# New issue orders for all five engines, and one buffer for the residual's x and the attention output, in a hybrid attention layer

## The chip, the cores and the metric

The kernel runs on one core of a Trainium2 chip. The metric is the device time of one execution in microseconds (us), median of several runs.

## What is computed

One layer of a hybrid decoder for 256 tokens of 1024 channels, all float32. From the reference, cut to what matters here:

```python
h = _rmsnorm(x, norm1_g[i])
proj = h @ w_in[i]
(q_a, k_c, v_c, k_s, v_s, k_w, v_w, g_nsa,
 q_b, k_b, v_b, g_ma, g_mb) = jnp.split(proj, SPLIT_POINTS, axis=-1)
...
y_a = _nsa_mixer(q_a, k_c, v_c, k_s, v_s, k_w, v_w, g_nsa, ...)
y_b = _dilated_mixer(q_b, k_b, v_b)
mixed = jax.nn.sigmoid(g_ma) * (y_a @ w_o_a[i]) + jax.nn.sigmoid(g_mb) * (y_b @ w_o_b[i])
x = x + mixed @ w_out[i]
h2 = _rmsnorm(x, norm2_g[i])
x = x + jnp.square(jax.nn.relu(h2 @ w_up[i])) @ w_down[i]
```

## The kernel before

All products run on TensorE with a split into two parts: a value is a rounded high part plus a remainder, and a product is three matmuls, high by high, low by high and high by low. The activations' parts are hT0 and hT1 at the first norm. hT0 is x times the gain, made by ScalarE (L415), and hT1 is its remainder, made by VectorE (L416), both per 256 columns of the four x pieces xg0 to xg3, which each come by their own transfer; xg0 carries the gains too. The factor of the root mean square, rs, is applied later, to the products.

The weights come in pieces of 128 x 768 (384 KB; the four of kv_w are 128 x 840, and 420 KB). Each is transferred into a `raw` tile, on ScalarE's DMA queue for the first four (kv_c) and on SP's for all others (L315); ScalarE casts it to the high part wh (L345; the first one is cast by VectorE in two halves, L349), and VectorE subtracts for the low part wl (L350). A tile's number is written behind its name: wl_216 is the low part that belongs to raw_86 and wh_215. TensorE's products of the first projection chunks (accumulators acc_149, acc_150, then others) are at L468 and L479 to L481; those of the compression network (hacc) are at L613 and L615.

For rs, ScalarE squares the x pieces (sx, L426), GpSimd adds the squares (L428), TensorE sums over channels, VectorE writes ss (L435), and GpSimd raises it to the power -1/2 (L436). GpSimd also makes six rope tables from gr and rope (L444, L447). dg (L994) are diagonal matrices of rs. The first y tiles (L573) are products that ScalarE scales with rs. A key chunk goes through norm and rope on VectorE, which ends in vk (L524), and is transposed by TensorE in three matmuls (L552). y, 8 KB in each partition, also names the attention output, whose last part is read by ScalarE (L959) and VectorE (L960); x1 (L1101), another 8 KB, is x once more, for the residual after w_out (L1116).

What sets the order: the program is written in one order, and a table ORDER then gives for each of the five engines the sequence in which its instructions are issued, as numbers of the instructions as written ("0+4" is 0, 1, 2, 3); `issue_order` ties each to the one ahead of it, without a semaphore. Each engine runs its sequence strictly in order, so an instruction that waits holds all that stand behind it, and that holds for the transfers issued by SP too: at most eight transfers of the kernel are in flight, and a further one waits for the landing of one ahead. A tile from one of the pools `big`, `tok`, `att` and `ps` has a place of its own, whatever tag it is given, since the wrapper `Own` makes the tag unique:

```python
    def tile(self, shape, dt, name, **_):
        self.n += 1
        return self.pool.tile(shape, dt, name=name, tag=f"{name}{self.n}", bufs=1)
```

## Time and profile before

| | |
|---|---|
| three runs | 459.05, 459.05, 459.7 us, median 459.05 us |
| the profiled execution | 458.8 us, with a span of 457.0 us from its first to its last instruction |
| granted TensorE clock, mean | 0.993 |
| busy, of the span | TensorE 445.6 us, VectorE 358.0 us, ScalarE 284.2 us, GpSimd 83.7 us |
| read from memory | 75.28 MB |

Instructions of one engine are issued in order, and a row of the timeline shows when it began and for how long it was busy; consecutive ones overlap a little, so two of 0.96 us may take 1.8 us together. Matmuls are pipelined: of two that stand at 51.05 and 51.23 the pitch, 0.18 us, is the work, and 0.34 us is the time that one takes through the array. The time in brackets is how long the engine was idle ahead of the row, and on whom it waited. TensorE is the engine that sets the end, in the MLP alone for more than 200 us, which start with the products of L983 to L985.

### The profile page before, as it was taken

What the parts mean: (1) busy time and instruction counts of PE and PEld (TensorE: products, weight loads), DVE (VectorE), ACT (ScalarE), POOL (GpSimd) and SP (SyncE); (2) the same over time, 40 slices, a digit from 0 to 9 for tenths busy, and PEclk for the clock granted to TensorE, in tenths of its full rate; (3) what the DMA queues carried; (4) which work ended last, traced back from release to release, by engine and by line L of the source; (5) the groups of instructions that cost most, each with busy time, mean ns of one, the idle gap of its engine ahead of it and who ended that gap; (6) DMA issues with size and microseconds to landing.
All of it is one profiled execution on the core that took longest, in us unless ns stands there. A gap on an engine that the chain in (4) does not pass through costs nothing.

```text
span 457.0 us, 9071 instructions
## 1 busy us (share of the span) xinstructions
PE 445.6 (98%) x3413; PEld 431.1 (94%) x3413; DVE 358.0 (78%) x654; ACT 284.2 (62%) x622; POOL 83.7 (18%) x92
## 2 busy tenths in 40 slices
PE   4999999999999999999999999999999999999996
PEld 4999899899999999898999999999999999999996
DVE  3989999999999998899999886886856654555440
ACT  4855677678999778876775555665665634433330
POOL 2712121313041000200000001796322300000000
PEclk9799999999999999999999999999999999999999
DMA  8974586725535522541521647666666667677620
GB/s 304 367 244 146 154 287 181 236 89 167 157 105 141 171 70 71 175 140 68 162 82 42 199 128 231 201 193 186 205 184 195 183 187 210 185 216 199 179 78 13
DMA packets 29484, 76.92 MB, mean 168 GB/s; under 512 B 3664, under 2 KB 5120, under 8 KB 29312
## 3 DMA queue, kind: packets, MB, share of 16 engines
q1 hardware_dynamic: 28864, 74.77, 54.7%
q10 hardware_dynamic: 576, 1.57, 1.0%
q8 instruction: 27, 0.44, 0.4%
q14 instruction: 17, 0.14, 0.1%
HBM read 75.28 MB, written 1.05 MB: 167 GB/s over the span
## 4 chain that ended last, share of the span: by engine, by line
PE 93%; DVE 2%; ACT 2%; DMA 2%; issue 0%; ACTq 0%
PE acc L983 19%; PE acc L985 19%; PE acc L984 19%; PE acc L480 6%; PE acc L481 6%; PE acc L479 6%; PE tp L709 3%; PE acc L468 2%; DMA raw<-in_kv_c 2%; PE sp L754 1%; PE pvo L721 1%; ACT wh L345 1%; PE pvo L723 1%; PE tp L552 1%; PE dsp L920 1%; PE hacc L615 1%
## 5 line engine op out<-in xcount | busy, mean ns | idle before, releaser
L350 DVE TENSOR_TENSOR wl<-raw,wh 128x768 fp32r<-128x768 f32 (+2 forms) x183 | 177.6, 979 | 61.7 <-ACT wh L345 57.2
L345 ACT CAST wh<-raw 128x768 fp32r<-128x768 f32 (+1 forms) x182 | 149.6, 833 | 102.1 <-PE acc L984 74.5
L983 PE MATMUL acc<-u,wh 128*128 128x256 f32 x256 | 71.6, 280 | 0.0
L984 PE MATMUL acc<-u,wh 128*128 128x256 f32 x256 | 71.6, 280 | 0.0
L985 PE MATMUL acc<-u,wl 128*128 128x256 f32 x256 | 71.5, 279 | 0.0
L984 PE MATMUL acc<-h,wh 128*128 128x256 f32 x256 | 69.0, 280 | 0.0
L983 PE MATMUL acc<-h,wh 128*128 128x256 f32 x256 | 69.0, 279 | 0.0
L985 PE MATMUL acc<-h,wl 128*128 128x256 f32 x256 | 66.1, 279 | 0.0
L480 PE MATMUL acc<-wl,hT 128*128 128x384 f32 (+1 forms) x164 | 55.1, 350 | 0.3 <-DVE wl L350 0.3
L479 PE MATMUL acc<-wh,hT 128*128 128x384 f32 (+1 forms) x164 | 54.7, 348 | 0.0
L481 PE MATMUL acc<-wh,hT 128*128 128x384 f32 (+1 forms) x164 | 54.6, 347 | 0.0
L1159 POOL TENSOR_TENSOR r<-r 128x256 f32<-128x256 f32 x32 | 27.7, 866 | 128.7 <-ACT r L1158 127.5
L985 PEld LDWEIGHTS acc<-u,wl 128*128 128x128 f32 x256 | 48.2, 188 | 0.0
L983 PEld LDWEIGHTS acc<-u,wh 128*128 128x128 f32 x256 | 48.1, 188 | 0.0
L984 PEld LDWEIGHTS acc<-u,wh 128*128 128x128 f32 x256 | 48.1, 188 | 0.0
L983 PEld LDWEIGHTS acc<-h,wh 128*128 128x128 f32 x256 | 47.6, 188 | 0.0
L984 PEld LDWEIGHTS acc<-h,wh 128*128 128x128 f32 x256 | 47.4, 188 | 0.0
L985 PEld LDWEIGHTS acc<-h,wl 128*128 128x128 f32 x256 | 45.8, 188 | 0.0
L502 POOL TENSOR_TENSOR st<-st,nhalf 128x6 f32<-128x6 f32 (+1 forms) x16 | 21.6, 1348 | 92.8 <-DVE st L501 65.7
L984 PE MATMUL acc<-hT,wh 128*128 128x256 f32 x128 | 36.1, 293 | 0.0
L985 PE MATMUL acc<-hT,wl 128*128 128x256 f32 x128 | 35.9, 293 | 0.0
L983 PE MATMUL acc<-hT,wh 128*128 128x256 f32 x128 | 35.1, 290 | 0.0
(212 smaller groups left out, 986.9 us busy)
## 6 DMA issues: line engine op xcount, KB each, us to landing
raw<-in_cells SPq DMA_DIRECT2D x128, 384.0 KB, 3.4
raw<-in_cw SPq DMA_DIRECT2D x10, 384.0 KB, 3.2
raw<-in_q_a SPq DMA_DIRECT2D x8, 384.0 KB, 3.8
raw<-in_q_b SPq DMA_DIRECT2D x8, 384.0 KB, 3.4
raw<-in_k_b SPq DMA_DIRECT2D x8, 384.0 KB, 3.2
raw<-in_v_b SPq DMA_DIRECT2D x8, 384.0 KB, 3.1
raw<-in_kv_w SPq DMA_DIRECT2D x4, 420.0 KB, 6.7
raw<-in_kv_c ACTq DMA_DIRECT2D x4, 384.0 KB, 7.0
```

What stands on the lines that cost most here:

```text
L345: nc.scalar.copy(hi[:, :m], src)
L350: nc.vector.tensor_sub(lo[:, :m], src, f(hi[:, :m]))
L468: nc.tensor.matmul(acc[t][:, :n], hT[h][:, k, t * 128:(t + 1) * 128], w[:, kk * n:(kk + 1) * n], start=h == 0 and k == 0 and w is hi, stop ...
L479: nc.tensor.matmul(o, hT[0][:, k, ts], hi[:, c], start=k == 0, stop=False)
L480: nc.tensor.matmul(o, hT[0][:, k, ts], lo[:, c], start=False, stop=False)
L481: nc.tensor.matmul(o, hT[1][:, k, ts], hi[:, c], start=False, stop=k == 7)
L502: nc.gpsimd.tensor_tensor(st[:, 1, :h], st[:, 0, :h], nhalf[:, :h], op=OP.pow)
L709: nc.tensor.transpose(pt[0:rows, i * 128:(i + 1) * 128], s, ident)
L983: nc.tensor.matmul(o, hi, a[0][k], start=start, stop=False)
L984: nc.tensor.matmul(o, hi, a[1][k], start=False, stop=False)
L985: nc.tensor.matmul(o, lo, a[0][k], start=False, stop=stop)
L1159: mul = nc.gpsimd.tensor_mul(r, r, r)
```

## The change

Two things are changed. The tiles y and x1 now come from the pool directly, with the same tag and one buffer, so that they share a place; x1's transfer then has to wait for the last reader of y. And all five sequences of the table ORDER are replaced. The instructions themselves, their number as written included, are the same, except for that place. The core of the diff:

```diff
     "SP": """
-1 0 2 4 3 9+2 104 15 13 12 16 11 19 14 20 18 5 17 6 8 7 21+83 105+60 166 165 167+4 172 171 173+5 179 178
-180+4 185 184 186+4 191 190 192+5 198 197 199+2""",
+0+3 11 13 9 3 16 19 15 4 20 12 8 14 10 17 5 18 6+2 21+80 104 101+3 105+60 166 165 167+4 172 171 173+5 179
+178 180+4 185 184 186+4 191 190 192+5 198 197 199+2""",
     "ACT": """
-0+4 6 10 13 9 4+2 7+2 11 16 15 14 17 12 19+2 25+4 18 21 47 22 24 35 48 36 23 49 38 41 37 58 42 29+2 32+2 43
...
+0+4 5 4 9 8 7 10 6 15+2 11 13+2 25 19+2 12 26+2 17 28 23 18 24 21 54 29 22 35 32+2 36 30 47 38 58 31 50 48+2
...
     "DVE": """
-3 2 4+2 12 0+2 6+2 13+2 16 22 18 15 19 23 8+3 24+2 17 11 77 79 20 58 21 36 59 37 60 64+2 62 66 39 61 47 63
...
-    st_["y"] = once([128, 8, S], F32, "y")
+    st_["y"] = big.pool.tile([128, 8, S], F32, name="y", tag="y", bufs=1)
...
-    x1 = big.tile([128, 8, S], F32, name="x1", tag="y", bufs=1)
+    x1 = big.pool.tile([128, 8, S], F32, name="x1", tag="y", bufs=1)
     nc.sync.dma_start(x1.rearrange("p k s -> p (k s)"), A["xg"][:, 16:])
```

Twelve lines fewer stand in the table after, so a line of the program after is the line before less 12.

**The start, on ScalarE and VectorE.** ScalarE, behind the four transfers of kv_c that it issues, before:

```order
L345 CAST wh_160<-raw_83 128x768
L426 ACTIVATE sx1_181<-xg1_77 128x512
L345 CAST wh_215<-raw_86 128x768
L426 ACTIVATE sx0_180<-xg0_76 128x512
L415 ACTIVATE hT0_137<-xg0_76 128x256 x2
L415 ACTIVATE hT0_137<-xg1_77,xg0_76 128x256 x2
L426 ACTIVATE sx2_182<-xg2_78 128x512
L415 ACTIVATE hT0_137<-xg2_78,xg0_76 128x256 x2
```

After:

```order
L403 ACTIVATE hT0_137<-xg0_76 128x256 x2
L414 ACTIVATE sx0_180<-xg0_76 128x512
L403 ACTIVATE hT0_137<-xg1_77,xg0_76 128x256 x2
L414 ACTIVATE sx1_181<-xg1_77 128x512
L333 CAST wh_160<-raw_83 128x768
L403 ACTIVATE hT0_137<-xg2_78,xg0_76 128x256 x2
L414 ACTIVATE sx2_182<-xg2_78 128x512
L333 CAST wh_215<-raw_86 128x768
```

VectorE at its start, before:

```order
L349 CAST wh_155<-raw_80 128x384 x2
L350 TENSOR_TENSOR wl_156<-raw_80,wh_155 128x768
L350 TENSOR_TENSOR wl_161<-raw_83,wh_160 128x768
L350 TENSOR_TENSOR wl_216<-raw_86,wh_215 128x768
L416 SCALAR_TENSOR_TENSOR hT1_138<-xg0_76,hT0_137 128x256 x2
L416 SCALAR_TENSOR_TENSOR hT1_138<-xg1_77,xg0_76,hT0_137 128x256 x2
L350 TENSOR_TENSOR wl_220<-raw_89,wh_219 128x768
```

After:

```order
L404 SCALAR_TENSOR_TENSOR hT1_138<-xg0_76,hT0_137 128x256 x2
L337 CAST wh_155<-raw_80 128x384 x2
L338 TENSOR_TENSOR wl_156<-raw_80,wh_155 128x768
L404 SCALAR_TENSOR_TENSOR hT1_138<-xg1_77,xg0_76,hT0_137 128x256 x2
L338 TENSOR_TENSOR wl_161<-raw_83,wh_160 128x768
L404 SCALAR_TENSOR_TENSOR hT1_138<-xg2_78,xg0_76,hT0_137 128x256 x2
L338 TENSOR_TENSOR wl_216<-raw_86,wh_215 128x768
```

On ScalarE the scalings (hT0) of xg0 and xg1 moved ahead of the casts and the squares; on VectorE the remainders (hT1) of xg0 moved to the head, those of xg1 ahead of wl_161 and wl_216, and those of xg2 ahead of wl_216 and wl_220.

**The transfers that SP issues first.** Before:

```order
L314 DMA xg1_77<-in_xg 128x512
L314 DMA xg0_76<-in_xg 128x528
L314 DMA xg2_78<-in_xg 128x512
L315 DMA raw_92<-in_kv_s 128x768
L314 DMA xg3_79<-in_xg 128x512
L315 DMA raw_102<-in_kv_w 128x840
L381 DMA gr_104<-in_gr 128x768
L1101 DMA x1_3396<-in_xg 128x2048
L393 DMA cw2_114<-in_cw2 128x256
```

After:

```order
L302 DMA xg0_76<-in_xg 128x528
L302 DMA xg1_77<-in_xg 128x512
L302 DMA xg2_78<-in_xg 128x512
L372 DMA rope_106<-in_rope 128x256
L377 DMA rowm_110<-in_rowm 128x1
L303 DMA raw_102<-in_kv_w 128x840
L302 DMA xg3_79<-in_xg 128x512
L303 DMA raw_116<-in_kv_w 128x840
```

x1 (1024 KB) stood eighth; it now stands behind 101 others, three places ahead of where it is written, with weight pieces before and behind it. gr, which all rope tables need, went from seventh to sixteenth, and xg0 from second to first.

**The transposes of the key tile vk_439, on TensorE, and the end of vk_439 on VectorE.** hT0_137 is x's high part, blk1_375 the input of the compression network, tp_614 the transposed tile. TensorE before:

```order
L480 MATMUL acc_578<-wl_413,hT0_137 128x384
L481 MATMUL acc_578<-wh_412,hT1_138 128x384
L479 MATMUL acc_578<-wh_482,hT0_137 128x384
L480 MATMUL acc_579<-wl_519,hT0_137 128x384
L552 MATMUL tp_614<-ident_100,vk_439 128x128 x3
L480 MATMUL acc_578<-wl_483,hT0_137 128x384
L552 MATMUL tp_722<-ident_100,vk_571 128x128 x3
```

After:

```order
L467 MATMUL acc_763<-wh_826,hT0_137 128x384
L601 MATMUL hacc_811<-wh_816,blk1_375 96x256
L603 MATMUL hacc_811<-wl_817,blk1_375 48x256
L467 MATMUL acc_764<-wh_685,hT0_137 128x384
L601 MATMUL hacc_811<-wh_816,blk1_375 96x256
L603 MATMUL hacc_811<-wl_817,blk1_375 48x256
L540 MATMUL tp_614<-ident_100,vk_439 128x128 x3
L601 MATMUL hacc_811<-wh_816,blk1_375 96x256
```

VectorE before:

```order
L350 TENSOR_TENSOR wl_501<-raw_394,wh_500 128x768
L350 TENSOR_TENSOR wl_519<-raw_416,wh_518 128x768
L524 TENSOR_TENSOR vk_439<-t1_434,st_430 128x384
L524 TENSOR_TENSOR vk_571<-t1_566,st_562 128x384
L350 TENSOR_TENSOR wl_581<-raw_418,wh_580 128x768
```

After:

```order
L621 TENSOR_TENSOR z0_780<-tp_777,z1_781 128x96
L499 TENSOR_TENSOR t1_734<-t1_734,t2_735 128x384
L338 TENSOR_TENSOR wl_817<-raw_677,wh_816 128x768
L623 SCALAR_TENSOR_TENSOR z1_781<-z1_781,z0_780 128x96
L512 TENSOR_TENSOR vk_439<-t1_434,st_430 128x384
L338 TENSOR_TENSOR wl_827<-raw_689,wh_826 128x768
```

Before, tp_614 is the 231st of TensorE's matmuls in the trace (a transpose is one, the ten at the start are counted) and vk_439 the 78th step of VectorE; after, the 319th and the 96th. The matmuls and steps between moved ahead of them.

## Rows read from the trace of the kernel before

**Rows 1.** The page, part 1: busy us (share of the span) xinstructions.

```profile
PE 445.6 (98%) x3413; PEld 431.1 (94%) x3413; DVE 358.0 (78%) x654; ACT 284.2 (62%) x622; POOL 83.7 (18%) x92
```

**Rows 2.** The chain of waits from 0 to 13 us: start us, us, what.

```profile
1.65 7.63 DMA raw<-in_kv_c
...
9.30 0.83 ACT wh L345
10.13 0.53 ACT sx L426
10.66 0.41 ACT hT L415
```

**Rows 3.** The timeline from 4.5 to 12 us: start, us, instruction [idle before <-releaser].

```profile
5.01 0.63 DVE L349 CAST wh<-raw 128x384 fp32r<-128x384 f32 x2 [5.01 <-DMA raw<-in_kv_c]
...
6.98 0.19 POOL L440 COPY g<-xg 128x8 f32<-128x8 f32 x1 [4.58 <-DMA xg<-in_xg]
...
7.52 0.83 ACT L345 CAST wh<-raw 128x768 fp32r<-128x768 f32 x1 [3.39 <-DMA raw<-in_kv_c]
...
11.12 1.33 PE L468 MATMUL acc<-wh,hT 128*128 128x384 f32 x3 [4.09 <-ACT hT L415]
```

**Rows 4.** DMA issues up to 1.15 us: KB each, median us to landing.

```profile
xg<-in_xg SPq DMA_DIRECT2D x1, 256.0 KB, 4.1
```

**Rows 5.** Stretches, all engines: us, busy (instructions) of each engine, granted clock, DMA.

```profile
11.10:17.10 6.00, 5.98 (x18) 5.64 (x19) 6.00 (x8) 6.00 (x12) 4.10 (x3) 0.50 1.04 389
17.10:24.00 6.90, 6.90 (x44) 6.81 (x43) 6.87 (x10) 3.58 (x5) 5.63 (x7) 1.00 0.98 345
```

**Rows 6.** Stretches, VectorE alone: us, busy (instructions), granted clock, DMA.

```profile
5.00:11.10 6.10, 3.48 (x6) 0.93 1.02 394
11.10:52.70 41.60, 40.01 (x76) 0.93 0.68 224
52.70:140.00 87.30, 84.90 (x181) 1.00 0.60 181
```

**Rows 7.** The timeline of TensorE, 49 to 53 us.

```profile
49.66 0.28 PE L613 MATMUL hacc<-wh,blk 128*96 128x256 f32 x1
49.78 0.28 PE L615 MATMUL hacc<-wl,blk 128*48 128x256 f32 x1
...
51.05 0.34 PE L481 MATMUL acc<-wh,hT 128*128 128x384 f32 x1
51.23 0.34 PE L479 MATMUL acc<-wh,hT 128*128 128x384 f32 x1
51.87 0.44 PE L480 MATMUL acc<-wl,hT 128*128 128x384 f32 x1 [0.30 <-DVE wl L350]
52.42 0.52 PE L552 MATMUL tp<-ident,vk 128*128 128x128 f32 x3
```

**Rows 8.** The timeline of VectorE before those transposes.

```profile
49.99 1.81 DVE L350 TENSOR_TENSOR wl<-raw,wh 128x768 fp32r<-128x768 f32 x2
51.73 1.01 DVE L524 TENSOR_TENSOR vk<-t,st 128x384 f32<-128x384 f32 x2
```

**Rows 9.** The timeline of GpSimd, five of the rope tables.

```profile
18.44 5.24 POOL L444 TENSOR_TENSOR ropeg<-rope,gr 128x256 f32<-128x256 f32 x5 [1.26 <-DMA rope<-in_rope]
```

**Rows 10.** The timeline of VectorE beside GpSimd's sums and tables.

```profile
15.95 2.99 DVE L350 TENSOR_TENSOR wl<-raw,wh 128x768 fp32r<-128x768 f32 x2
18.86 2.73 DVE L416 SCALAR_TENSOR_TENSOR hT<-xg,xg,hT 128x256 fp32r<-128x256 f32 x3
21.52 1.57 DVE L350 TENSOR_TENSOR wl<-raw,wh 128x840 fp32r<-128x840 f32 x1
...
23.70 3.10 DVE L350 TENSOR_TENSOR wl<-raw,wh 128x840 fp32r<-128x840 f32 x3
```

**Rows 11.** The timeline: VectorE's last read of y; ScalarE's cast behind x1's place.

```profile
244.93 0.43 DVE L960 SCALAR_TENSOR_TENSOR yb<-y,yb 128x256 fp32r<-128x256 f32 x1 [0.48 <-ACT yb L959]
...
253.96 0.84 ACT L345 CAST wh<-raw 128x768 fp32r<-128x768 f32 x1
```

More of the change, by code (lines that the diff above doesn't have):

```diff
@@ L120 @@
     "SP": """
-1 0 2 4 3 9+2 104 15 13 12 16 11 19 14 20 18 5 17 6 8 7 21+83 105+60 166 165 167+4 172 171 173+5 179 178
-180+4 185 184 186+4 191 190 192+5 198 197 199+2""",
+0+3 11 13 9 3 16 19 15 4 20 12 8 14 10 17 5 18 6+2 21+80 104 101+3 105+60 166 165 167+4 172 171 173+5 179
+178 180+4 185 184 186+4 191 190 192+5 198 197 199+2""",
     "ACT": """
[15 rows of a table removed]
-474 473 475+3 479 478 481 480 482 484 483 485+3 489 488 491 490 492 494 493 495+3 499 498 501 500 502+38""",
-    "DVE": """
[20 rows of a table removed]
-635+2 634 637+4 643 641 644 642 645+4 650+2 649 652+2""",
-    "PE": """
[60 rows of a table removed]
-2575+17 2597 2592+3 2598 2595 2599+20 2620 2619 2621+767""",
[15 rows of a table added]
+495+3 499 498 501 500 502+38""",
+    "DVE": """
[20 rows of a table added]
+650+2 649 652+2""",
+    "PE": """
[48 rows of a table added]
+1870+2 1893+3 1899+4 1872 1896 1903+4 1873+2 1897+2 1907+1481""",
     "POOL": """
-28 25 2 15 14 0+2 7 3+3 11+2 10 9 8 6 13 18 17 16 19+3 23+2 22 26+2 34+2 38 37 40 29 39 30 33 31 36 32 42 41
-45+5 44 50+5 56 55 57+4 62 61 63+11 43 74+14""",
+15 14 28 25 1 0 2 7 3+3 13 12 11 6 9 8 10 18+2 16+2 20+2 23 22 24 26+2 34+2 38 29 39 30 37 40 33 36 31+2
+41+11 53 52 54+34""",
 }
```

175 rows, old and new, of the table ORDER are left out of this document.

## The prediction

> **What bounds the kernel now.** I read the page's busy times first, then the chain of waits over the start, then the timeline there, then stretches of busy time, then the places further on where TensorE waits. TensorE is busy for 445.6 us of the 457.0 us span [rows 1]; so 11.4 us of the span are not TensorE work, and no change of order alone can win more. The profiled execution took 458.8 us, that is 1.8 us outside the span and 0.25 us under the median of the three runs (459.05). I make the sum on 458.8 and carry the difference to the median.
>
> Most of the 11.4 us is the start. The chain from the first issue to the first real matmul is a weight transfer (kv_c) to 9.28, then ScalarE's cast of it, then a square of x, then the first hT0 scaling, and then the matmul [rows 2]: ScalarE's queue holds hT0 of xg0, which is all that the first matmul lacks, behind two casts and two squares. The timeline shows that none of this is needed: xg0 had landed by 6.98 (GpSimd's small copy starts then), VectorE had cast the first weight piece at 5.01, ScalarE sat idle for 3.39 us until a weight at 7.52, and TensorE idled 4.09 us until 11.12 [rows 3]. A second loss follows: after this idle time the granted clock was 0.50 (1.2 GHz) from 11.10 to 17.10, so TensorE started 18 matmuls in 6.00 us, against 44 in 6.90 us at 1.00 (2.4 GHz) [rows 5]. At full rate 18 matmuls of 0.18 us (one starts at 51.05, the next at 51.23 [rows 7]) are 3.2 us, so 2.8 us went there, and TensorE stands as if it had started at 13.9 with the full clock.
>
> The other bound is VectorE, which makes the low half (wl) of every weight and hT1. It did only 3.48 us of work in six instructions before 11.1, and then 40.01 us in 41.60 [rows 6]: from the start to 52 us it is nearly always busy, and TensorE runs on what it hands over. The place that shows it is 51.87, where TensorE waits for a wl, and 52.42, the transposes of vk [rows 7], which VectorE finished only just before (two wl from 49.99, two vk from 51.73 [rows 8]). Past it VectorE is idle 2.4 us of 87.3 [rows 6], so it is close but no longer last.
>
> **The change, part by part.** *ScalarE's and VectorE's start.* hT0 and hT1 of xg0 now stand first on both engines, and xg0 is the first transfer on SP. The first transfer there took 4.1 us from its issue at 0.73 [rows 4], so xg0 lands at about 4.8; at worst at 6.98 as before [rows 3]. From 4.8, ScalarE's two hT0 (0.41 each by the chain [rows 2]) end at 5.7; VectorE's two hT1 (0.91 each, three took 2.73 [rows 10]) run to 7.3, its two half casts (0.63 [rows 3]) to 7.9. The first half cast is there at 7.6, so the first real matmul moves from 11.12 to about 7.6. The matmuls that follow use hT1 and wl in the order in which VectorE now makes them: wl of the first piece (0.87) to 8.8, hT1 of xg1 to 10.6, one wl, hT1 of xg2 to 13.2, three wl, the first hT1 of xg3 at 16.9. The product with that last one has 8.0 us of TensorE work ahead of it in the new order (matmuls counted in the order, 0.18 us each), so TensorE then stands as if started at 8.9 instead of 13.9: 5.0 us better. The low clock does not add to it: even if another 18 matmuls took 6.0 us [rows 5], the same count gives 10.8 at most, which the next step exceeds.
>
> *What VectorE lets through.* It is last further on, so its own lead counts. By 11.1 it will have done two hT1, the two half casts, one wl, two more hT1 and half a wl: 1.8 + 0.6 + 0.9 + 1.8 + 0.5, about 5.6 us, against 3.48 [rows 6]: 2.1 us ahead. It gives some back: its dg (from rs) now stand ahead of two wl, and ScalarE's first y likewise waits for rs ahead of a cast. rs needs GpSimd's pow after ss, which VectorE writes at about 22, so the two engines stand for about 2.0 us there; before, VectorE lost about 1.6 us in all between 11.1 and 52.7 (41.60 - 40.01 [rows 6]), which now falls away in part. I take 0.3 to 0.5 us as the net price, 0.4; if rs came in time it would be nothing. The lead is then 1.7 to 1.8 us.
>
> *The tight place.* The transposes of vk_439 (52.42 [rows 7]) go back on TensorE past 44 matmuls of 384 columns at 0.18 us (51.05 to 51.23 [rows 7]) and 39 of 256 columns at 0.12 us (49.66 to 49.78 [rows 7]): 7.7 + 4.7 = 12.4 us of work that no longer waits for them. On VectorE vk_439 goes back past nine wl and nine smaller steps. Two wl take 1.74 us from start to start (49.99 to 51.73 [rows 8]), so nine are 7.8; the nine are up to 0.50 each (two vk took 1.01 [rows 8]), with three short ones, 3.3 us in all. 12.4 - 11.1 = 1.3 us more room. Other products there (wl for the compression matmuls, the next transposes) have, by the same count, nearly the same room, so no more than this comes. Lead and room, 1.8 + 1.3, make 3.1 us, less than the 5.0 that the start gives: **-3.1 us** to the region about 50 us.
>
> *From 100 to 140.* There the new order puts projections closer behind their wl than the old one: counted the same way, the smallest room of VectorE against TensorE is 1.3 us less than before. Before, TensorE was some 2 us behind what VectorE allowed there (VectorE's idle time is 2.4 us [rows 6]); with 3.1 us gained, 1.8 of them VectorE's own, about 0.5 us falls back: **+0.5**, between 0 and 1.5. From 140 to 250 the small rearrangements of transposes and attention steps move instructions by a few places; TensorE had short waits there in both directions, and I take 0, within 1.5 either way. The MLP is in written order in both and its part is equal.
>
> *x1 in y's buffer.* The 1 MB transfer leaves the start, where it stood eighth on SP; at 389 GB/s [rows 5] it had delayed all behind it by 2.7 us, which brings the kv_w weights forward. It now waits for y's last reader, VectorE's yb at 244.93 + 0.43 [rows 11], and holds the cell weights queued behind it on SP. Issued at about 242.6 with the gain, it takes some 2.7 us, and the 384 KB behind it 1.1 us more: 246.4, some 247 with the issue. ScalarE casts that piece at 253.96 [rows 11], about 251 with the gain. Four us of cover: **0**. If the cover were gone, each us late would cost one.
>
> *Rest.* GpSimd's tables and sums beside VectorE's wl. Before, a table took 1.05 us (5.24 for five [rows 9]); beside them one wl of 840 columns took 1.57 us against 1.03 alone (3.10 for three), and a pair beside a sum took 2.99 where 1.9 was due [rows 10]: 0.5 and 1.1 us lost. In the new order three or four wl stand beside tables, at 0.5 us each, so 1.5 to 2.0 against 1.6: 0, within 1.
>
> The sum is -3.1 + 0.5 = -2.6 us: 456.2 on the profiled execution, **456.4 us** on the median.
>
> **The rivals.** *A: the start's gain is kept whole.* If VectorE's wl pass 52 us with no new waits and the 0.3 us waits of [rows 7] simply vanish, TensorE runs 4.5 to 5.0 us ahead: 454.2. For it: the new order is spread so that VectorE has wl for other products between. Against it: VectorE's 40.01 of 41.60 busy [rows 6], which leaves no reserve to win more than its own lead. *B: VectorE blocked by GpSimd.* If a wl is held for a whole table (1.05 us) instead of half, three of them lose 3.2 instead of 1.6 us, and the gain shrinks to about 1.0: 458.0. Against it: 0.5 us for the row of 1.57 [rows 10]; for it the pair of 2.99. The Trainium skill, page "SBUF — State Buffer", section "Who interferes with whom", says just this: a VectorE instruction with two SBUF inputs contends with a GpSimd instruction that reads SBUF, and the later one is fully blocked; by that rule the time would be B's, and the trace agrees only for part of the cases. *C: xg0 lands no earlier.* Moved to the head of SP it may still share the 16 engines with the four kv_c weights; landing at 6.98 it takes 2.1 us from VectorE's lead, which leaves 3.1 - 2.1 + 0.5: 458.5. Against it: the 4.1 us of the first transfer [rows 4]. *D, slower: rs comes late.* gr, which the tables need, is sixteenth on SP instead of seventh. Some 5.5 MB are queued up to it, at 389 GB/s 14.1 us, so it lands at about 18, and three tables (0.7 + 2 x 1.05) and the pow end before 22, when ss comes anyway. ScalarE's y and VectorE's dg wait on rs with all casts and wl behind them. Each us that rs is past 23.5 then costs one us of lead; with 3.1 us gained it turns to slower past about 26.5, that is, if gr landed after about 23. At rs 28 the time would be 460.5. Against it: the rates of 389 and 345 GB/s [rows 5], which would have to fall by a third.
>
> **How the numbers follow.** The forecast, -1.5 to -4 us, has 0.57; A 0.16; B and C 0.08 each; D 0.11. Less than 0.2%, 0.9 us, cannot be told from no change here. Half of B and C lies within it. So faster is 0.57 + 0.16 + 0.06, some 0.78, same 0.11, slower 0.11. The range goes from A's better end, 453.9, to C with its own uncertainty, 458.9, and leaves out D and the far end of A.
>
> **What would show it.** The first real matmul at about 7.6; VectorE's hT1 from about 5.4 and 5 to 6 us of work before 11.1; xg0 landed by 5; TensorE at vk_439's transposes about 3 us earlier for the same work; rs at about 23; x1 issued at about 242 and the cast behind it without idle time. I am wrong if TensorE waits longer than 1 us anywhere past 60 us, if rs is later than 26, or if VectorE's wl beside tables take 2 us.

## The result, and the profile after

The changed kernel takes 463.03 us (median of four runs, 462.92 to 463.3) against 459.05 us before (458.94 to 459.7): 1.0085 times as long, with an interval of 1.0067 to 1.0102. It is slower by 4.0 us, where 456.4 was predicted. Its profiled execution took 462.92 us; the view of the cores gives its span and granted clock, which is higher than before (0.993):

```profile
core 0: 461.1 us, clock 0.999
```

The beginning went as meant. The timeline from 4 to 14 us (start, us, instruction, in brackets the idle time ahead and its releaser) answers to [rows 3]:

```profile
5.22 0.91 ACT L403 ACTIVATE hT<-xg 128x256 fp32r<-128x256 f32 x2 [0.93 <-DMA xg<-in_xg]
...
5.77 0.89 DVE L404 SCALAR_TENSOR_TENSOR hT<-xg,hT 128x256 fp32r<-128x256 f32 x2 [5.77 <-ACT hT L403]
...
6.57 0.62 DVE L337 CAST wh<-raw 128x384 fp32r<-128x384 f32 x2
...
7.07 1.65 PE L456 MATMUL acc<-wh,hT 128*128 128x384 f32 x8 [0.58 <-DVE wh L337]
```

xg0 had landed by 5.22, VectorE began with hT1 at 5.77, and the first real matmul stands at 7.07 instead of 11.12. In the stretches of [rows 5] (us, busy time and instructions of TensorE, its weight loads, VectorE, ScalarE and GpSimd, granted clock, DMA share, GB/s) the half clock is gone:

```profile
11.10:17.10 6.00, 5.41 (x29) 4.48 (x28) 6.00 (x7) 4.69 (x8) 2.46 (x2) 1.00 1.05 386
17.10:24.00 6.90, 6.90 (x41) 6.81 (x42) 6.23 (x8) 1.64 (x3) 3.16 (x5) 1.00 0.92 320
```

In those of VectorE alone, which answer to [rows 6], it had done 5.30 us of work by 11.1 instead of 3.48:

```profile
5.00:11.10 6.10, 5.30 (x9) 1.00 1.04 404
11.10:52.70 41.60, 39.63 (x70) 1.00 0.70 232
```

So the gain was made and then lost. To see where, I take TensorE's **lateness**: the start of a matmul in the trace, less the work of all real matmuls that stand ahead of it in that kernel's order, each at its usual pitch at full clock. An engine that never waits keeps its lateness; each wait, each slow stretch adds to it. Since the two orders differ, "at 50 us" means after 50 us of work, and no particular matmul.

| us of TensorE work done | lateness before | after | difference |
|---|---|---|---|
| 0 | 11.12 | 7.07 | -4.1 |
| 20 | 14.11 | 9.60 | -4.5 |
| 30 | 14.19 | 11.21 | -3.0 |
| 50 | 15.59 | 13.33 | -2.3 |
| 100 | 16.19 | 14.57 | -1.6 |
| 140 | 16.80 | 17.21 | +0.4 |
| 250 | 23.19 | 24.08 | +0.9 |
| 300 | 23.66 | 24.92 | +1.3 |
| 420 | 24.73 | 29.05 | +4.3 |

The usual pitch of a shape is not one number, and the rows are good to about half a us: with the median pitch of each shape over both traces the differences are -4.5 at 20, -3.3 at 30, -2.3 at 50, -1.5 at 100, +1.2 at 140 and +0.6 at 250.

Three losses stand in it: 2.2 us from 20 to 50, 3.2 us from 50 to 250 (most of it from 100 to 140), 3.4 us from 250 to the end. A matmul at the same place in both programs says much the same without the table: the 1821st, in the residual's projection, began at 269.10 before and at 269.61 after, and the last one, in the down projection, at 452.86 and 457.00.

**The first loss** shows on VectorE, in two places. The first is beside GpSimd's tables. GpSimd's timeline after, with rs between two groups of tables:

```profile
17.99 0.59 POOL L435 TENSOR_TENSOR ropeg<-ropec,gr 48x128 f32<-48x128 f32 x1 [1.36 <-DMA gr<-in_gr]
18.54 1.44 POOL L432 TENSOR_TENSOR ropeg<-rope,gr 128x256 f32<-128x256 f32 x2
22.83 0.72 POOL L424 TENSOR_TENSOR rs<-ss,nhalf 128x2 f32<-128x2 f32 x1 [2.85 <-DVE ss L423]
23.51 2.14 POOL L432 TENSOR_TENSOR ropeg<-rope,gr 128x256 f32<-128x256 f32 x3
```

VectorE's timeline at the same time:

```profile
17.23 5.45 DVE L338 TENSOR_TENSOR wl<-raw,wh 128x840 fp32r<-128x840 f32 x4
...
23.59 1.46 DVE L982 TENSOR_SCALAR dg<-ident,rs 128x128 f32<-128x128 f32 x2 [0.63 <-POOL rs L424]
24.96 1.50 DVE L338 TENSOR_TENSOR wl<-raw,wh 128x768 fp32r<-128x768 f32 x1
```

Four wl took 5.45 us, two dg 1.46 and one wl 1.50. The view of the tile wl gives the four one by one (ns, shortest/median/longest):

```profile
L338 DVE TENSOR_TENSOR wl<-raw,wh x4: 947/1020/2694, 17.2 to 21.7; 128x840 fp32r<-128x840 f32 x3, 128x768 fp32r<-128x768 f32 x1
```

Three took 0.95 to 1.02 us, as a wl does with GpSimd idle, and one, which began at 18.17, took 2.69: GpSimd made three tables in a row from 17.99 to 19.97, and the wl did some 0.9 us of work behind them. The kernel before pays the same way, in other instructions. Three hT1 beside its tables (view of the tile hT):

```profile
L416 DVE SCALAR_TENSOR_TENSOR hT<-xg,xg,hT x3: 953/959/972, 18.9 to 20.6; 128x256 fp32r<-128x256 f32 x3
```

Two hT1 with GpSimd idle, at the start of the kernel after:

```profile
L404 DVE SCALAR_TENSOR_TENSOR hT<-xg,hT x2: 482/484/485, 5.8 to 6.2; 128x256 fp32r<-128x256 f32 x2
```

Added up from 5 to 28 us, what VectorE's instructions take beyond the time of their kind with GpSimd idle is 5.7 us before (3.1 beside sums, 2.6 beside tables) and 6.4 after (3.2 and 3.2). So this costs a lot in both kernels, and the new order added 0.7 us to it.

The second place stands in VectorE's timeline at 47.67, an idle time of 1.12 us:

```profile
47.67 0.96 DVE L338 TENSOR_TENSOR wl<-raw,wh 128x768 fp32r<-128x768 f32 x1 [1.12 <-ACT wh L333]
```

The chain of waits (start, us, what) says why:

```profile
41.24 0.96 DVE wl L338
42.25 4.45 DMA raw<-in_cw
46.81 0.84 ACT wh L333
```

ScalarE could not cast before a weight of the compression network, issued at 42.25, had landed at 46.7; and the chain puts ahead of that issue a wl of VectorE itself, which ended at 42.20. So it is a loop from VectorE over the transfer and ScalarE back to VectorE. In VectorE's own lateness (its time less its own work) the lead over the kernel before was about 3.4 us at 12 us of work, 2.0 at 20, 1.9 at 35 and 0.9 at 40.

**The second loss** has no large wait. The view of waits lists only one past 50 us, of 0.4 us, and it is in TensorE's timeline (384 columns have a pitch of 0.18 us here, so the second row is 0.56 us late):

```profile
124.63 0.34 PE L469 MATMUL acc<-wh,hT 128*128 128x384 f32 x1
125.36 0.51 PE L709 MATMUL pvo<-phi,vSW 128*128 128x512 f32 x1 [0.39 <-ACT P L769]
```

From 94 to 142 us of the trace the matmuls that start over 0.1 us late sum to some 2.6 us after and 0.7 us before; with the smaller ones the difference is 2.7 to 3.2 us, by the pitch that is taken as usual. TensorE is idle for only 0.56 us of it (not at all before), so how much is waiting and how much TensorE's own change from one shape to the next is not told apart here.

**The third loss** is in the MLP, where nothing waits at all. Both kernels have 120 us of TensorE work in 120 us, at a granted clock of 1.00, but not the same number of matmuls. The row of this stretch before (each count holds two that were already running at 320.00):

```profile
320.00:440.00 120.00, 120.00 (x1028) 120.00 (x1027) 69.61 (x90) 58.15 (x92) 13.89 (x18) 1.00 0.67 191
```

And after:

```profile
320.00:440.00 120.00, 120.00 (x1002) 120.00 (x1002) 67.33 (x87) 56.30 (x90) 14.20 (x17) 1.00 0.69 193
```

The pitch of equal matmuls, fp32r and 256 columns wide, is 117.06 ns in the mean before (mostly 116.67) and 120.0 ns after. A pitch is a mean here: at 120.0 every start is 120 ns behind the one ahead, at 116.67 they lie 113 to 120 ns apart. In the kernel after it changes at one place, the two float32 matmuls of the second norm (L1155; L1167 before). TensorE's timeline after, around it:

```profile
311.16 0.28 PE L973 MATMUL acc<-h,wl 128*128 128x256 f32 x1
...
312.45 0.28 PE L972 MATMUL acc<-h,wh 128*128 128x256 f32 x1
...
312.69 0.59 PE L1155 MATMUL tp<-sqs,ones 128*128 128x256 f32 x2
...
313.24 0.28 PE L972 MATMUL acc<-h,wh 128*128 128x256 f32 x1
...
314.56 0.28 PE L971 MATMUL acc<-h,wh 128*128 128x256 f32 x1
```

Eleven pitches take 1.29 us ahead of it (311.16 to 312.45), which is 117 ns each, and 1.32 us behind it (313.24 to 314.56), 120 ns each, and so it stays for 1198 matmuls: 1198 x (120.0 - 117.06) ns = 3.5 us.

**x1** did not wait for y. The rows of its line:

```profile
L1089 SPq DMA_DIRECT2D x<-in_xg x1: 328/328/328, 233.7 to 233.7; - x1
...
DMA to landing us min/median/max: 4.7/4.7/4.7
```

And VectorE's last read of y in its timeline, which answers to [rows 11]:

```profile
245.30 0.43 DVE L948 SCALAR_TENSOR_TENSOR yb<-y,yb 128x256 fp32r<-128x256 f32 x1 [0.48 <-ACT yb L947]
```

It was issued at 233.7 and landed 4.7 us later, at 238.4, before that read at 245.30. The common tag and single buffer did not make it wait for y's last reader, as the section on the change says they do. Part of y was even written at 244.4 (L956), behind the landing; in one place that would have overwritten x1. So the two hardly share a place, which is argued from these times, since no trace shows places.

### The profile page after: what moved, and what is told of

It is laid out like the page before. It is cut to its first block, busy times and chain, and to the rows that moved or that the text cites. A ratio compares the mean times of both kernels' runs of the same rounds, so it can differ in the third digit from the quotient of the medians.

```text
span 461.1 us, 9062 instructions
## 1 busy us (share of the span) xinstructions
PE 451.0 (98%) x3410; PEld 431.7 (94%) x3413; DVE 357.3 (77%) x654; ACT 284.5 (62%) x622; POOL 79.4 (17%) x92
## 4 chain that ended last, share of the span: by engine, by line
PE 86%; DVE 5%; ACT 2%; DMA 1%; issue 1%; POOL 0%; ACTq 0%; SPq 0%
PE acc L971 20%; PE acc L972 20%; PE acc L973 20%; PE acc L468 4%; PE acc L467 4%; PE acc L469 4%; PE tp L697 2%; DVE wl L338 2%; PE sp L742 1%; PE dsp L908 1%; DMA raw<-in_cw 1%; PE pvo L709 1%; PE pvo L711 1%; PE tp L540 1%; PE dpo L709 1%
## 5 line engine op out<-in xcount | busy, mean ns | idle before, releaser
L973 PE MATMUL acc<-h,wl 128*128 128x256 f32 x256 | 71.6, 281 | 0.0
L972 PE MATMUL acc<-h,wh 128*128 128x256 f32 x256 | 71.6, 281 | 0.0
L971 PE MATMUL acc<-h,wh 128*128 128x256 f32 x256 | 71.5, 282 | 0.0
L467 PE MATMUL acc<-wh,hT 128*128 128x384 f32 (+1 forms) x164 | 56.1, 353 | 0.0
L469 PE MATMUL acc<-wh,hT 128*128 128x384 f32 (+1 forms) x164 | 54.7, 347 | 0.6 <-DVE hT L404 0.6
L1147 POOL TENSOR_TENSOR r<-r 128x256 f32<-128x256 f32 x32 | 30.3, 949 | 129.7 <-ACT r L1146 129.6
L971 PEld LDWEIGHTS acc<-u,wh 128*128 128x128 f32 x256 | 48.9, 191 | 0.0
L972 PEld LDWEIGHTS acc<-u,wh 128*128 128x128 f32 x256 | 48.9, 191 | 0.0
L972 PEld LDWEIGHTS acc<-h,wh 128*128 128x128 f32 x256 | 48.4, 190 | 0.0
L973 PEld LDWEIGHTS acc<-h,wl 128*128 128x128 f32 x256 | 48.4, 190 | 0.0
L971 PEld LDWEIGHTS acc<-h,wh 128*128 128x128 f32 x256 | 48.3, 190 | 0.0
```

Source lines behind the costliest of these rows:

```text
L467: nc.tensor.matmul(o, hT[0][:, k, ts], hi[:, c], start=k == 0, stop=False)
L469: nc.tensor.matmul(o, hT[1][:, k, ts], hi[:, c], start=False, stop=k == 7)
L971: nc.tensor.matmul(o, hi, a[0][k], start=start, stop=False)
L972: nc.tensor.matmul(o, hi, a[1][k], start=False, stop=False)
L973: nc.tensor.matmul(o, lo, a[0][k], start=False, stop=stop)
L1147: mul = nc.gpsimd.tensor_mul(r, r, r)
```

## The experiments

The ratios, with their 95% intervals, are against the kernel before, timed beside each on the same chip. "Lateness" is the measure above. Where an edit puts parts of the two orders together, it is written as the diff of a few entries of ORDER.

### The start alone

`old_start` puts the new beginning on the kernel before: SP's first transfers, x1 late, the first 23 instructions of ScalarE, 17 of VectorE and 34 of TensorE.

```diff
     "SP": """
-1 0 2 4 3 9+2 104 15 13 12 16 11 ...
+0+3 4 3 9+2 15 13 12 16 11 ...
     "ACT": """
-0+4 6 10 13 9 4+2 7+2 11 16 15 ...
+0+4 5 4 9 8 7 10 6 15+2 11 13+2 25 ...
```

> The kernel before with the changed kernel's start alone: xg0 first on SP, x1's transfer late (places of its own), ScalarE's first 23 instructions, VectorE's first 17 and TensorE's first 34 in the new order, all else as before; ScalarE's y and VectorE's dg therefore stay behind the wl as before. First real matmul near 7.1 instead of 11.1. Theory V (VectorE's own lead is what lasts; the new body gives it up): about 2 us of lead at 50 us, most of it kept to 140 us since the old body has about 0.8 us of slack there, MLP at 117 ns: 456.7 to 457.7. Theory O (the lead is lost in any body): within 0.5 us of 459.0. If the MLP falls into the 120 ns pitch: 3.5 us more in either.

462.28 us, 1.0067 [1.005, 1.0084]: slower. In TensorE's timeline:

```profile
18.31 0.69 PE L479 MATMUL acc<-wh,hT 128*128 128x384 f32 x1 [6.13 <-ACT wh L345]
```

And the stretch from there, with its granted clock:

```profile
18.30:24.00 5.70, 5.42 (x18) 5.32 (x19) 3.74 (x3) 2.41 (x3) 4.42 (x4) 0.50 0.84 297
```

TensorE ran out at 12.2, waited 6.13 us for a cast that the spliced ScalarE order had put too late, and then ran at half clock (0.50, 1.2 GHz) until 27.5. The kernel ends 3.5 us later than the one before. So an early start alone is no gain: what follows must be there too. `old_start2` fits it better: the casts and the wl that the next products need are moved to where they are due.

```diff
     "ACT": """
-0+4 6 10 13 9 4+2 7+2 11 16 15 14 17 12 19+2 25+4 18 ...
+0+6 9 7+2 10 6 15+2 11 13 17 14 25 19+2 12 26+3 18 ...
     "DVE": """
-3 2 4+2 12 0+2 6+2 13+2 16 22 18 15 19 23 8+3 ...
+0+2 3 2 4 6+2 5 12 14 16 22 13 15 18+2 23 8+3 ...
```

> The kernel before with the new start fitted to its own order of products: xg0 first on SP, x1's transfer late (places of its own); on ScalarE hT0 of xg0 and xg1 ahead of the casts, then kv_s0's and kv_w0's casts as early as before; on VectorE hT1 of xg0 at the head, of xg1 behind the first wl; on TensorE only the first two matmuls of the squares' sum three products later. Everything from about 20 us on is in the old order. (The first splice failed since TensorE's old order wants kv_s0 early and ScalarE's new order casts it late: 6.1 us of waiting.) Theory V (VectorE's lead lasts, the new body's order loses it): TensorE 4 us earlier at 20 us, 1.5 to 2.5 us earlier at 50 us, the same 1.5 to 2.5 at 140 and 250 us, the MLP at 116.7 to 117.1 ns: 456.4 to 457.5. Theory O (the old body takes it back too): 458.5 to 459.3.

459.30 us, 1.0 [0.9988, 1.0012]: no difference. It is 4 to 5 us early until 8 us of work, waits for 0.86 and 1.86 us at 17 to 21, and gets a lower clock behind that; at 20 us of work its lateness is 14.82, no better than before (14.11). The second wait in TensorE's timeline:

```profile
21.14 1.04 PE L480 MATMUL acc<-wl,hT 128*128 128x420 f32 x2 [1.86 <-DVE wl L350]
```

And the stretch around it:

```profile
17.10:24.00 6.90, 4.23 (x16) 3.82 (x17) 6.87 (x10) 2.56 (x3) 5.93 (x7) 0.71 0.86 327
```

The granted clock was 0.71 in this stretch in the mean, against 1.00 in the kernel after: it fell to 0.50 (1.2 GHz) at 20.0, within the second wait, and stayed there until 26.9.

### GpSimd's tables

`new_memset` replaces five rope tables by a constant, so that GpSimd writes them without reading.

```diff
-            eng.tensor_mul(tab, rope, gr[:, :, kind][:, None].to_broadcast([128, NT, 2, 64]))
+            eng.memset(tab, 1.0)
```

> The changed kernel with GpSimd's five rope tables filled with ones by a memset, which reads nothing, in place of the product of rope and gr. Theory B (VectorE's wl and dg are held by GpSimd's reads: the wl of 840 columns took 1.36 us each beside two tables, and dg with the next wl 2.9 us beside three): VectorE gains 1.0 to 2.4 us between 17 and 27 us, rs comes at 22 or earlier, and TensorE's lead at 50 us grows by 0.5 to 1.5 us. Without B, rows and time stay.

462.04 us, 1.0063 [1.0048, 1.0078]. VectorE's rows for the same instructions as in the kernel after:

```profile
16.78 4.04 DVE L338 TENSOR_TENSOR wl<-raw,wh 128x840 fp32r<-128x840 f32 x4
...
22.31 0.88 DVE L982 TENSOR_SCALAR dg<-ident,rs 128x128 f32<-128x128 f32 x2 [0.64 <-DMA raw<-in_q_a]
23.64 0.96 DVE L338 TENSOR_TENSOR wl<-raw,wh 128x768 fp32r<-128x768 f32 x1 [0.46 <-ACT wh L333]
```

4.04 instead of 5.45 us, 0.88 instead of 1.46, 0.96 instead of 1.50: with constants VectorE is 2.5 us shorter there, and the longest of the four wl takes 1.21 us instead of 2.69. The dg are still held, by GpSimd's writes alone: with GpSimd idle they took 0.28 us each, in the kernel before at 26.8. TensorE is 0.95 us earlier by 50 us of work (12.38 against 13.33) and keeps that to 140 (16.25 against 17.21), but 0.37 of it stands from its first matmul on (6.70 against 7.07), ahead of any table; some 0.6 us come from the tables. More does not get through, since the wl that waited for 1.12 us at 47.67 now waits for 1.75. The run also tells something of the second loss. The gap shown above stands in this kernel 0.97 us earlier and is as long:

```profile
123.66 0.33 PE L469 MATMUL acc<-wh,hT 128*128 128x384 f32 x1
124.39 0.50 PE L709 MATMUL pvo<-phi,vSW 128*128 128x512 f32 x1 [0.40 <-ACT P L769]
```

A lead did not shorten it. So TensorE does not lose this because the work ahead is late as a whole. I read it as a loop of short steps, here from TensorE to ScalarE's P and back, that is as long as the order around it makes it.

`new_wl3` asks the same from the other side: three wl at 68.7 to 71.3 us are cut to 8 columns, and TensorE reads the high part in their place, which takes 2.9 us of work from VectorE.

```diff
+            if n in (32, 33, 34):
+                nc.vector.tensor_sub(lo[:, :8], src[:, :8], f(hi[:, :8]))
+                parts.append((hi, hi))
+                continue
```

> The changed kernel, but three of VectorE's wl (at 68.7 to 71.3 us) take 8 of 768 columns, and TensorE uses the high part in place of these low parts: the same matmuls, 2.5 us less on VectorE. Theory V (VectorE bounds the region from 100 to 140 us in the new order, where 2.6 us of TensorE's lead went): TensorE stands 1.2 to 2 us earlier for the same work at 130 us. Theory S (the losses there are ScalarE's waits and TensorE's own switching): no more than 0.4 us earlier. The MLP's pitch may change with it, so the comparison is made at 140 us.

463.67 us, 1.0102 [1.0087, 1.0117]: no gain. VectorE is busy for 26.71 us from 60 to 90 instead of 29.56, and TensorE still loses the same from 97 to 140; its lateness from 90 to 140 is even 0.5 us worse, for which I have no cause. VectorE's throughput is not the bound there, although the prediction's +0.5 for this place was computed from it.

### The new order up to a point, the old one behind it

These kernels take, on all five engines, what had begun in the new kernel's trace by T us in the new order, and the rest in the old one; y and x1 have their own places.

```diff
     "SP": """
-1 0 2 4 3 9+2 104 15 13 12 16 11 ...
+0+3 11 13 9 3 16 19 15 4 20 12 8 14 10 17 5 18 6+2 ...
     "ACT": """
-0+4 6 10 13 9 4+2 7+2 11 16 15 ...
+0+4 5 4 9 8 7 10 6 15+2 11 13+2 25 ...
...
```

> The new order on all engines for what had begun by 30 us in the changed kernel's trace, the old order for the rest; y and x1 in places of their own. Theory O (the new order of 97 to 250 us costs by itself some 2.6 us): TensorE 4 us earlier at 30 us, 1.5 to 2.3 at 55 us, and that is kept to 250 us within 0.5; with the MLP near 117 ns, 456.8 to 457.7. Theory E (who arrives early waits there in any order): the lead is 0 to 0.5 us at 140 us; 458.7 to 459.2.

> As cut30, cut at 52 us. Theory O: the lead of 2.2 us at 52 us is kept to 250 us: 456.5 to 457.5 with the MLP near 117 ns. Theory E: 458.7 to 459.2.

> As cut30, cut at 80 us. Theory O: the lead of 1.9 us at 80 us is kept to 250 us: 456.8 to 457.8 with the MLP near 117 ns. Theory E: 458.7 to 459.2. If cut30 and cut52 keep their lead and this one doesn't, the place is between.

`rev80` is the reverse: the old order up to 80 us, the new one behind it.

> The old order for what had begun by 80 us in the trace of before, the new order behind it. Theory O: no lead at 80 us and TensorE 2.0 to 2.8 us later than before at 250 us; with the MLP near 117 ns 461 to 462, at 120 ns 464.5 to 465.5. Theory E: no later than before at 250 us.

| T | us | ratio [95%] |
|---|---|---|
| 30 | 458.60 | 0.9984 [0.9975, 0.9993] |
| 52 | 461.17 | 1.0059 [1.0036, 1.0082] |
| 80 | 457.42 | 0.9961 [0.9951, 0.9972] |
| reverse, 80 | 466.86 | 1.0171 [1.0155, 1.0186] |

The old order after 80 us keeps a lead: `cut80` is 1.5 us ahead of the kernel before at 80 us of work and 1.5 at 250. The new order loses without one: `rev80` is 1.7 us behind at 80 (0.6 of it stands from 20 us of work on, the rest comes at the joint) and 4.3 at 250, so 2.6 us went in the new middle with nothing to lose; the changed kernel goes from 1.9 ahead to 0.6 behind, 2.5 us, over the same work (all six with the median pitch of each shape). Both agree: the second loss belongs to the new order from 80 to 250 and is no lead given back. `cut80` came out as theory O has it, `rev80` 1.4 us above its upper end. `cut30` and `cut52` say nothing on it, because a joint has a price of its own: at 52 TensorE waits 2.85 us at 55.72 for a vk that one part puts late and the other wants early, and at 30 it waits 2.61 us at 37.97 for a vk, behind which the granted clock was 0.50 from 39.3 to 42.7, so that 0.8 us of a lead of 4.5 are left. So I tried three more joints.

> As cut80, cut at 66 us. Theory O: the changed kernel is 2.0 us ahead at 66 us; less what the joint costs (1.2 us of waits in cut80), 0.8 to 2.0 us remain at 250 us: 457.0 to 458.2.

> As cut80, cut at 72 us. Theory O: 1.9 us ahead at 72 us, less the joint: 457.0 to 458.2.

> As cut80, cut at 96 us, just ahead of the stretch in which the new order lost 2.6 us. Theory O: 1.7 us ahead at 96 us, less the joint: 457.2 to 458.4; where the joint costs nothing 457.2.

| T | us | ratio [95%] |
|---|---|---|
| 66 | 457.08 | 0.9945 [0.993, 0.996] |
| 72 | 457.88 | 0.9965 [0.995, 0.9979] |
| 96 | 457.84 | 0.9968 [0.9955, 0.9981] |

All three came out within what was expected, and the joint at 66 is faster than both kernels: 2.25 us under the kernel before. Its lateness is 12.84 at 50 us of work, 14.24 at 80, 15.03 at 140 and 21.61 at 250, so 1.6 us of the gain of the start passes through the old middle; the 1821st matmul begins at 267.30 (269.10 before, 269.61 after). Its MLP has a pitch of 116.67 ns throughout, which against the mean of 117.06 before is worth another 0.4 us; the stretch of the MLP in this kernel:

```profile
320.00:440.00 120.00, 120.00 (x1030) 120.00 (x1030) 68.34 (x89) 58.56 (x91) 14.34 (x17) 1.00 0.69 191
```

### The pitch in the MLP

Is it TensorE's order there? `new_oldmlp` gives the kernel after the old order of TensorE from the 1950th matmul as written, `old_newmlp` gives the kernel before the plain written order.

```diff
-1870+2 1893+3 1899+4 1872 1896 1903+4 1873+2 1897+2 1907+1481""",
+1870+2 1893+3 1899+4 1872 1896 1903+4 1873+2 1897+2 1907+109 2019 2016 2020 2017+2 2021+15 ...
```

> The changed kernel with one edit: TensorE's matmuls from the residual on (those written from number 1950 on) stand in the order of the kernel before, which swaps neighbours within the up projection; all else as changed. In the profile of the changed kernel every matmul of the MLP behind the norm's float32 matmul (313 us) starts exactly 120 ns after the one ahead; before, 116.7 ns is the usual pitch. Theory P (the order of TensorE's instructions in the MLP sets the pitch): the pitch returns to 116.7 to 117.8 and the time falls by 3.0 to 3.8 us, to about 459.5. Theory A (the places of the tiles in memory, which the allocator made anew, set it): 120 ns stays and the time stays at 463. Theory F (the pitch is whatever phase the pipeline falls into after an interruption): either, with no tie to the edit.

> The kernel before with one edit: TensorE's matmuls written from number 1950 on in plain written order, as in the changed kernel. Theory P: the pitch behind the norm's matmul is 120 ns and the time rises by 3 to 3.8 us, to about 462.5. Theory A: the pitch stays at 116.7 and the time at 459. Theory F: either.

461.24 us, 1.0049 [1.0034, 1.0064], and 458.91 us, 1.0 [0.9991, 1.001]. The kernel before keeps its pitch of 117.0 with either order; the kernel after goes from 120.0 to 118.67, a third value. So TensorE's order in the MLP is not the cause by itself (theory P): the old one does not bring 116.67 back, nor the new one 120.0. `new_probe` looks at this by itself: six extra matmuls, of 64, 192, 256 (float32), 128, 256 (float32) and 64 columns, stand in the MLP of the kernel after.

```diff
+        if j in (18, 22, 26, 30, 35, 37):
+            n = {18: 64, 22: 192, 30: 128, 37: 64}.get(j)
+            if n:
+                nc.tensor.matmul(pq[:, 0:n], h2[0][:, 0, 0:128], h2[0][:, 1, 0:n], start=True, stop=True)
+            else:
+                nc.tensor.matmul(pq[:, 0:S], ones, sq[:, 0], start=True, stop=True)
```

> The changed kernel with six extra matmuls in the MLP that write a bank nobody reads: of 64, 192 and 128 columns in one pass, and two of 256 columns in float32 (two passes), at about 328, 340, 352 (float32), 364, 382 (float32) and 405 us. They cost some 0.1 us each, the float32 ones 0.5. Theory F (the pitch is a rhythm that the matmul pipeline falls into and keeps until something interrupts it): the pitch changes behind one or more of them, from 120.0 to one of the values seen (116.7, 117.3, 117.8, 118.7), and stays constant between them; where all later pieces ran at 117, the time would be 461. Theory A (tile places) or a slower supply: 120.0 returns at once behind each.

One execution took 462.98 us. The stretches between the extra matmuls, all at a clock of 1.00 and never idle (the one behind 128 columns is left out):

```profile
315.00:327.00 12.00, 12.00 (x102) 12.00 (x102) 10.11 (x13) 7.97 (x16) 3.97 (x5) 1.00 0.65 200
329.00:338.00 9.00, 9.00 (x79) 9.00 (x79) 5.70 (x8) 5.21 (x10) 2.98 (x4) 1.00 0.68 189
340.00:350.00 10.00, 10.00 (x87) 10.00 (x86) 6.26 (x9) 6.00 (x12) 3.25 (x4) 1.00 0.68 187
352.00:362.00 10.00, 10.00 (x85) 10.00 (x85) 5.99 (x8) 6.12 (x12) 2.52 (x3) 1.00 0.67 176
402.00:422.00 20.00, 20.00 (x171) 20.00 (x170) 9.38 (x11) 8.29 (x10) 0.00 (x0) 1.00 0.70 192
424.00:440.00 16.00, 16.00 (x139) 16.00 (x138) 8.53 (x11) 6.02 (x8) 0.00 (x0) 1.00 0.71 193
```

The pitches behind them are 120.0 at first, then 117.3 (behind 64 columns), 118.7 (192), 120.0 (float32), 120.0 (128), 118.7 (float32) and 117.3 ns (64). Each stretch holds one pitch, and a foreign matmul sets a new one; the same kind may set two values (float32: 120.0 and 118.7). `new_one64` uses it: one matmul of 64 columns at 328 us.

```diff
+        if j == 18:
+            nc.tensor.matmul(pq[:, 0:64], h2[0][:, 0, 0:128], h2[0][:, 1, 0:64], start=True, stop=True)
```

> The changed kernel with one extra matmul of 64 columns in the MLP, at 328 us, whose output nobody reads; nothing else. With several of them the pitch behind this first one was 117.3 ns in place of 120.0. Theory F (a rhythm that holds until something interrupts it): 117.3 ns from 328 us to the end; of the 1,080 matmuls there each is 2.7 us/1000 shorter, 2.9 us, less 0.1 for the extra one: 460.1 to 460.4. If the pitch goes back to 120: 463.

460.45 us, 1.0028 [1.0017, 1.0039]. The pitch is 120.02 ns ahead of it and 117.33 behind it, through 1078 matmuls; 1078 x 2.69 ns = 2.9 us, and the kernel's distance to the one before, 4.0 us, is now 1.4, 2.6 less. The same stretch of the MLP:

```profile
320.00:440.00 120.00, 120.00 (x1023) 120.00 (x1023) 68.90 (x89) 57.66 (x91) 14.33 (x17) 1.00 0.69 195
```

### y and x1

`new_own` gives the kernel after separate places for y and x1; `old_share` gives the kernel before the common tag and moves x1 to its late place.

```diff
-    st_["y"] = big.pool.tile([128, 8, S], F32, name="y", tag="y", bufs=1)
+    st_["y"] = once([128, 8, S], F32, "y")
```

> The changed kernel with y and x1 in places of their own again, orders as changed. That x1's transfer waits for y was priced at nothing: time within 0.5 us of the changed kernel's 463.0, and no wait around 245 us that goes away. Theory A: the places of the tiles change, so the MLP's pitch may return to 116.7 and the time to 459.5. Theory P: 120 ns stays.

> The kernel before with only y and x1 in one place, and x1's transfer moved to where the changed kernel has it on SP (it has to be, since it now waits for y). With 1 MB less in the first 17 us, kv_w and kv_s land up to 2.7 us earlier; VectorE, which bounds the region up to 52 us, has its raws already, so I expect 0 to -0.7 us: 458.3 to 459.1. Theory A: the MLP's pitch may become 120 ns, and the time 462.5.

462.56 us, 1.0074 [1.0059, 1.0089], and 459.30 us, 1.0012 [1.0001, 1.0022]. Neither shows a wait at 245, and `new_own` issues x1 at 232.9 behind a wait of 6.3 us on SP, where the kernel after issues it at 233.7 behind one of 6.2: separate places change nothing there. `new_own` has a lateness of 12.45 at 40 us of work instead of 13.21, and still a pitch of 120.0. About 0.3 us of this stands from the first matmul on (6.79 instead of 7.07), and 0.37 comes where VectorE waits for the cast of 46.8: the idle time there is 0.75 us instead of 1.12. `old_share` is 0.8 us later from 12 to 200 us of work, with a pitch of 116.67. What makes these differences was not followed further; it is not a wait for y.

### The old order for the last part

`new_tail` takes the old order from the last attention steps on, on TensorE, VectorE, ScalarE and GpSimd.

```diff
     "ACT": """
...
-362 318 351 347+2 350 363 357+2 364+7 373 371+2 ...
+362 318 363+2 348 347 350+2 357+2 365+4 370 369 371+3 ...
```

> The changed kernel with the old order on TensorE, VectorE, ScalarE and GpSimd from the last attention steps (about 230 us) to the end; y and x1 share as changed. If the pitch comes from the order of the end on all engines: 116.7 ns behind the norm's matmul, and 3.5 us less than the changed kernel, 459.3 to 459.8. If it comes from what stands ahead: 118.7 to 120.0 and 461.3 to 463.

471.20 us, 1.0259 [1.0241, 1.0276]. The joint costs some 11 us by 250 us of work, with waits of 2.9, 2.6 and 1.1 us and a granted clock of 0.83 from 240 to 250, so the time says nothing. The pitch does: it is 118.6, so the old order of these four engines from 230 us on does not bring 116.67 back.

Over all runs the pitch goes with the order of what stands ahead. The eleven kernels that have the old order on all engines past 96 us, up to the MLP, stand at 116.67 to 117.1 ns: the one before, `old_start`, `old_start2`, `old_share`, `old_newmlp` and the six cuts. The seven that have the new order past 80 us to the end stand at 120.0: the one after, `new_own`, `new_memset`, `new_wl3`, `rev80`, and `new_probe` and `new_one64` up to their first extra matmul. `new_oldmlp` and `new_tail` stand between. So the value is not drawn anew in each kernel, but what in the order sets it is not shown.

## Why the prediction failed, step by step

- **The start, right.** "The first real matmul moves from 11.12 to about 7.6": 7.07. It is half a us earlier because two hT1 took 0.89 us together; the 0.91 that the prediction took for one is that of three which stood beside tables [rows 10]. xg0 by 5 (5.2), VectorE's 5 to 6 us of work ahead of 11.1 (5.30) and rs at about 23 (GpSimd made it from 22.83 to 23.5) came as written. The lateness fell by 4.5 us at 20 us of work, the forecast was 5.0. The step allowed for a half clock at the new start; there was none.
- **What VectorE lets through, mis-sized.** The lead was taken as 1.8 at the tight place. It was 1.9 at 35 us of VectorE work but 0.9 at 40: VectorE waited 1.12 us at 47.67 for a cast that waited for a transfer. The prediction counted VectorE's work and never asked when that weight could be issued and would land. The sum at 50 us is -2.3 instead of -3.1; what is left for the room, 2.3 - 0.9 = 1.4, is near the 1.3 of the forecast, but it is a remainder and was not measured by itself.
- **GpSimd beside VectorE, right in the difference, too small in its parts.** "1.5 to 2.0 against 1.6: 0, within 1" was a difference, and it came out at +0.7; the parts were 6.4 and 5.7 us, sums included. The rule of the Trainium skill, page "SBUF — State Buffer", section "Who interferes with whom", which carried rival B, is borne out: the wl of 2.69 us was held until the last of three tables was done. But instructions were held like that before the change too (0.96 us for an hT1 of 0.48), and so the rule takes little from the gain.
- **From 100 to 250, far too small.** "About 0.5 us falls back", and from 140 "I take 0, within 1.5": 0.9 us behind at 250, from 1.6 ahead at 100. I had counted the room of VectorE against TensorE, and `new_wl3` shows that this is no bound there. What is lost is in late starts of TensorE, none above 0.6 us, and the largest is no shorter with a lead (`new_memset`); that they are short loops over ScalarE, VectorE and TensorE whose length the order sets is my reading of that one, and not shown for the rest. `rev80` and the joints show that it is a price of the new order itself. Which of its many rearrangements cost it was not taken apart.
- **The MLP, "its part is equal", the largest miss.** It is not "in written order in both": the kernel before swaps neighbours in the up projection. That cost nothing (`old_newmlp`, 117.0 ns and no difference in time). The work is equal, the pitch was not: 3.5 us. The step took for granted that equal matmuls back to back take equal time. The trace of before already had more than one pitch in it (a mean of 117.06, mostly 116.67), and the prediction had no term for it.
- **x1, right by luck.** The price was 0, and four us of cover were named. In fact x1 was issued 11.6 us ahead of y's last read and waited for nothing of y.
- **The rivals.** C did not occur (xg0 landed by 5.2), nor D (rs in time), and the slower outcome came from a mechanism that no rival had. "I am wrong if TensorE waits longer than 1 us anywhere past 60 us" did not show it: no such wait exists, and the time was lost all the same, in gaps too small for the view of waits and in a pitch that no view of waits can show. Rival B's mechanism is there, as said above, in both kernels.
- **Slips that decided nothing.** TensorE's 445.6 busy us hold the 2.8 us that the half clock cost, so 11.4 us were not the most that an order could win. Rival C's 458.5 is -3.1 + 2.1 + 0.5, not the sum as written, and rival D's 460.5 leaves out the +0.5.

By the terms: -2.3 to 50 us (forecast -3.1), +0.7 to 100 (0), +2.5 to 250 (+0.5), +3.4 to the end (0): +4.3 by lateness, +4.1 between the two profiled executions.

## What to carry to other kernels

A lead at the start reaches the end only if the order behind it has no losses of its own, so follow the lateness of the bound engine over the whole kernel, and price a new order stage by stage; half of one order joined to half of another, at the right place, was better here than either. Where an engine is 100% busy, divide the time by the number of equal instructions as well: a busy share can't tell 116.7 from 120.0 ns. For an instruction moved early, ask not only for the engine that makes its operand but for the landing of the weight behind it, and for what must end before that transfer can be issued. And look at the longest instruction of a group, not only at its sum: "four wl in 5.45 us" was three as always and one held for 1.7 us.

## What was not expected of the hardware

Equal matmuls back to back (fp32r, 256 columns, granted clock 1.00, TensorE never idle) settle into one of several steady pitches, 116.67, 117.3, 118.6 to 118.7 or 120.0 ns, keep it for up to 1198 matmuls, and take another after a foreign matmul: between the ends, 1.7 us per 500 matmuls. All but 120.0 are means of uneven distances. What chooses the value is open: it goes with the order of the whole kernel, and not with TensorE's order in the MLP alone, the places of y and x1, or the granted clock, each of which was changed or compared. Second, a 1 MB transfer in the middle of the weight stream took 4.7 us to land, where I had reckoned 2.7 from the rate of the start.
